# Weight splits on VectorE instead of GpSimd outside DeltaNet's heads two to six, and a new order at the end of DeltaNet and of GLA

## The chip, the cores and the metric

The kernel runs on one core of a Trainium2 chip. The metric is the device time of one execution in microseconds (us); of several executions the median counts. The engines are TensorE (PE, matrix products; PEld is its weight loading), VectorE (DVE), ScalarE (ACT), GpSimd (POOL) and SyncE (SP), which issues the DMAs. Each engine works off its own queue in order.

## The reference, cut to what matters

Two transformer-like blocks run one after the other in float32 over 256 tokens (stream x) and 256 context tokens (stream c) of width 1024. The first block has two layers of attention with a Fourier and a convolution branch. The second has a DeltaNet layer and a GLA layer. Each layer ends with a feed-forward network of width 4096.

```python
h = modulate(rms_norm(x, g), shift, scale)       # for x and for ctx
# DeltaNet, 8 heads: q, k, v, z, a, b = h @ w_in (q, k, v through a short convolution)
for d in range(2):                               # forward and backward in time
    oc, state = gated_delta_rule(qc, kc, vc, ...)      # context first
    ox, _     = gated_delta_rule(qx, kx, vx, ..., state)
y = (rms_norm(o, norm_g) * silu(z)) @ w_out      # per head, then summed over heads
# GLA, 4 heads: the same with a gated linear recurrence, results for x alone
x = x + gate * y
x = x + gate2 * (square(relu(modulate(rms_norm(x, g2), ...) @ w1)) @ w2)
```

## The kernel before

*Products in two halves.* Every float32 weight tile of 128x1024 numbers arrives by DMA (`wr`), ACT casts it to a shortened format (`wh`, line 307), and DVE or POOL subtracts that from the original to get the rest (`wl`, line 308, "the split"). The activations are split likewise (line 295). A product is then three matmuls per 128 rows of the depth, so 24 for one weight tile over eight depth blocks: high by high, high by low, low by high (lines 316 to 318; they are 512 columns wide for both streams, 256 for one). Raw tiles have three buffers, `wh` and `wl` two each, and four in the feed-forward blocks.

*Who splits.* `weight(pool=True)` puts the split on POOL, and so does `self.pool_lo`, which `pools` sets for the whole of DeltaNet. Of the calls outside DeltaNet these have `pool=True`: the first four weights of each of the four feed-forward blocks (line 561), the two first weights of each mixer that `follow` loads ahead, and six weights at GLA's start.

*DeltaNet.* The mixer runs head by head, in a software pipeline written out by hand. In iteration `hd`: `merge` (inverts the head's triangular matrices), `steps` (four steps of the recurrence over chunks of 128 tokens; the context's two chunks are final after the second), `prepare` and `tokens` for the next head, `write_out` of the head before (its product with `w_out`, added to the running sum `xs` by `finish`, line 659), `scale` (sum of squares on ACT, then a reciprocal root on DVE in some ten short operations, lines 432 to 438, and a multiplication of the results `ot`, line 1416), `project` two heads ahead, and `readout` (transposes of `ot` on PE, a multiplication by the gates, a split), then `gates` of the next head. In the last iteration there is nothing left to prepare, so `late` makes 24 small parts of three matmuls each: the last head's second gate and the write-out of head seven. `between` hands one or two of them out between the matmuls of `merge` and `steps`; the rest runs after `scale` is issued. Then `readout`, and `write_out` for head eight, one stream after the other, with each stream's norm for the feed-forward block behind it (`then`, the `follow` function).

*GLA.* It runs by heads as well: `values` and the gate logits of the next head, `readout` of the head before, `gate` and `prepare` of the next head, then `finish` of this one, which makes the output in a PSUM tile `po` (one buffer), scales it into `ot` (one buffer, line 1676). The last `readout` is issued inside the final output product (`tail`).

*Order.* On each engine the instructions stand in an order that the framework plans before the run from the program's order and its own estimates of durations. `self.tc.issue_after(i)` keeps what is issued under it behind instruction i in that plan. The hardware then waits by semaphores only.

Of the kernel before, what the change touches and what calls it, by code (L numbers as in the profile page):

```python
# [204 lines left out]
class Net:  # L205
# [91 lines left out]
    def weight(self, src, into=None, pool=False, ahead=False):  # L297
        shp = list(src.shape)
        raw = self.wp.tile(shp, F32, tag="wr", bufs=self.nr_, name="wr")
        self.nc.sync.dma_start(raw, src)  # L300
        wp, nw = (self.wp2, 4) if self.wp2 and not ahead else (self.wp, self.nw)
        if into:
            hi, lo = into
        else:
            hi = wp.tile(shp, F32R, tag="wh", bufs=nw, name="wh")
            lo = wp.tile(shp, F32R, tag="wl", bufs=nw, name="wl")
        self.nc.scalar.copy(hi, raw)  # L307
        (self.nc.gpsimd if pool or self.pool_lo else self.nc.vector).tensor_tensor(lo, raw, hi.bitcast(F32), ALU.subtract)  # L308
        return hi, lo
# [10 lines left out]
    def lin(self, src, rhs, n0, n1, w=None, pool=False):  # L320
        w = w or self.weight(src, pool=pool)
        ps = self.mm_ps()
        self.mm3(ps[:, : n1 - n0], w, rhs, n0, n1)
        return ps[:, : n1 - n0]
# [194 lines left out]
    def follow(self, f, xs, S, gs, mod, shch, tag, win=None):  # L519
        f.update(h=self.rows16(), ws=None)  # L520

        def then(sv, y=None):
            if win and not f["ws"]:
                f["ws"] = [self.weight(w, pool=True, ahead=True) for w in win]
# [28 lines left out]
    def ffn(self, xs, g, w1, w2, mod, tag, streams, ys=None, h=None, quota=0, every=1, S=None, scales=None, before=None, then=None):  # L553
        one = len(streams) == 1
        with ExitStack() as st:
            self.pools(st, dict(n=(8, 256), h=3, acc=(4, 256), sq=(4, 256), rs=(1, 258)), dict(a=2, md=1, mm=5), 12 if one else 18, "a", quota)
            self.wp2 = self.lo
            if S is not None:
                S.update(acc={}, new=lambda n: self.t("acc", n), tmp=lambda n: self.t("sq", n))
            self.load_ahead(1)  # L560
            ws = [self.weight(self.a[w1][m], pool=True) for m in range(4)]
            self.background(1 if every == 2 else 0)
            self.load_ahead()
            self.every, self.slots = every, 0
            nS = None
# [4 lines left out]
            self.mlp(xs, h, ws, w1, w2, mod, 5, streams, S, scales or {"xc"[v]: 1.0 for (_, _, v) in streams}, before, then, nS)  # L570
            self.background(999)
            self.wp2 = None


    def mlp(self, xs, h, ws, w1, w2, mod, gch, streams, S, scales, before, then, nS):
        nc = self.nc
        n = 256 * len(streams)
        for s in range(4):
# [3 lines left out]
            for m in range(0, 8, 2):  # L582
# [88 lines left out]
    def pools(self, st, sb, ps, nr, pm, quota=0, pool_lo=False, nwm=2, wide=4, low=()):  # L671
        self.n += 1
        self.pool_lo = pool_lo
# [394 lines left out]
    def deltanet(self, xs, mod, h, ws, first):  # L1068
# [249 lines left out]
        def merge(hd, c, parts):  # L1318
# [30 lines left out]
        def steps(hd, c, parts):  # L1349
# [4 lines left out]
            for step in range(4):  # L1354
                Sn = ap.tile([P, 512], F32, tag="S", bufs=2, name="S") if step < 3 else None
                for d in range(2):
# [31 lines left out]
                    self.between(parts, i.ins, 2 if step == 3 else 1)  # L1388
# [13 lines left out]
                S = Sn  # L1402
            return ot

        def scale(c, ot):
            ss = sp.tile([P, 4, 2], F32, tag="ss", name="ss")
            jk = junk()
            for ch in range(4):
                for v in range(2):
                    nc.scalar.activation(jk, ot[ch // 2][:, 256 * (ch % 2) + P * v : 256 * (ch % 2) + P * v + P], AF.Square,  # L1410
                                         accum_out=ss[:, ch, v : v + 1])
            nc.vector.scalar_tensor_tensor(ss, ss, 1.0 / 128, c["aq"].unsqueeze(2).to_broadcast([P, 4, 2]), ALU.mult, ALU.add)
            so = self.rsqrt(ss.rearrange("p c v -> p (c v)"), [P, 8], "o")
            for p in range(2):
                o = ot[p].rearrange("p (c i) -> p c i", i=P)
                nc.vector.tensor_tensor(o, o, so[:, 4 * p : 4 * p + 4].unsqueeze(2).to_broadcast([P, 4, P]), ALU.mult)
# [11 lines left out]
        def write_out(hd, og, S=None, then=None):  # L1428
            ws = [self.weight(a["dwout"][hd, mq]) for mq in range(2)]
            for sv in st if S else [(0, 512, 0)]:  # L1430
                for m in range(8):
                    c = slice(P * (m % 4), P * (m % 4) + P)
                    wh, wl = ws[m // 4]
                    ps = self.mm_ps()[:, : sv[1] - sv[0]]
                    self.mm3(ps, (wh[:, :, c], wl[:, :, c]), og, sv[0], sv[1])
                    if S:
                        self.finish(xs, m, ps, mod, 2, sv, S, dict(x=1.0, c=1.0))
                    else:
                        for s2 in st:
                            self.finish(xs, m, ps[:, s2[0] : s2[1]], mod, 2, s2, None, None)  # L1440
                if then:
                    then(sv)
# [5 lines left out]
        og, parts = None, iter(())  # L1448
        for hd in range(8):
            if hd == 7:  # L1450
                parts = late(zs, og)
            merge(hd, c, parts)
            ot = steps(hd, c, parts)
            if hd < 7:
                nxt = prepare(hd + 1, *proj)
            if 0 < hd < 7:
                write_out(hd - 1, og)
            if hd < 7:
                tokens(nxt)
# [4 lines left out]
            elif hd == 6:  # L1464
                zn = [gate(7, 0)]
# [5 lines left out]
            if hd < 6:  # L1471
                zs = gates(hd + 1)
            elif hd == 6:
                zs = zn
            if hd < 7:
                c = nxt
# [4 lines left out]
        write_out(7, og, S, f["then"])  # L1481
# [4 lines left out]
    def gla(self, xs, mod, h, ws):  # L1486
# [46 lines left out]
        w3 = self.weight(win[2], [vtile().rearrange("p b n -> p (b n)").rearrange("p (k m) -> p k m", k=8).bitcast(F32R) for _ in range(2)], pool=True)  # L1533
# [5 lines left out]
        for m in range(4):  # L1539
            ps = self.lin(win[1 + m], h, 0, 512, w3 if m == 1 else None, True) if m else ps1  # L1540
# [6 lines left out]
        for m in range(4):  # L1547
            ps = self.lin(win[5 + m], h, 0, 256, None, m<3)
# [7 lines left out]
        def values(hd):  # L1556
            w = [self.weight(a["gwv"][hd, kh], pool=False) for kh in range(2)]
# [15 lines left out]
        def gate(hd):  # L1573
            zs = []
            for m in range(2):
                ps = self.lin(win[9 + 2 * hd + m], h, 0, 256, None, False)
# [121 lines left out]
        for hd in range(4):  # L1698
            if hd < 3:
                vn = values(hd + 1)  # L1700
                c1 = next(cg)
            if ot is not None:
# [6 lines left out]
            if hd < 3:  # L1709
                cur, vt, zs = nxt, vn, zn  # L1710

        def last():
            with self.tc.issue_after(self.mark.ins):
                og.extend(readout(3, ot, zo))
# [8 lines left out]
    def run(self):  # L1723
# [8 lines left out]
        if not skip:  # L1732
            fng = None
            y = None
            for l in range(2):
                with ExitStack() as st:
# [7 lines left out]
                    if l == 0:  # L1744
# [34 lines left out]
                        def early():  # L1779
                            self.background(2)  # L1780
                            ws = [self.weight(a["win_0"][m], pool=False) for m in (8, 9)]
# [24 lines left out]
                else:  # L1806
# [3 lines left out]
                    def before(s):  # L1810
# [6 lines left out]
                        if s == 2.5:  # L1817
# [4 lines left out]
                            f["ws"] = [self.weight(a["dwin"][m], pool=True, ahead=True) for m in range(2)]  # L1822
# [40 lines left out]
        with ExitStack() as st:  # L1863
            self.pools(st, dict(g=3, e=(5, 256)), dict(b=2, a=3, mm=3), 4, "b", pool_lo=True)
# [10 lines left out]
        self.ffn(xs, "fg_0", "f1_0", "f2_0", mods2[0][0], "4", both, None, h, 12, 4, S, None, before, lambda sv: f["then"](sv))  # L1875
        self.dump("slay0", xs)
        with ExitStack() as st:
            h = 256
            sb = dict(n=(6, h), low=1, k=4, q=(4, h), z=(4, h), kE=(2, h), kt=(2, h), S=(4, h), qe=(4, h), Ao=(1, h), part=2, A=(2, P), ot=1)
# [42 lines left out]
```

## Time and profile before

| | |
|---|---|
| median of 3 runs | 2655.13 us (2652.54 to 2656.1) |
| profiled execution | 2648.67 us |
| its span | 2646.9 us |
| mean granted clock of PE | 0.977 of full speed |
| PE busy | 2503.5 us, 95% |
| DVE busy | 1648.9 us, 62% |
| ACT busy | 1133.1 us, 43% |
| POOL busy | 370.3 us, 14% |

The profile is of one execution, recorded by the hardware; its span lies within that execution's time. "Busy" is the union of the recorded instructions on an engine. Matmuls overlap in the records, so their mean duration is longer than the distance from one to the next. PEclk is the clock that PE was granted as a share of full speed, 2.4 GHz; 0.5 is the lower level, 1.2 GHz. On the time axis the first block takes about 0 to 1000 us, DeltaNet 1000 to 1852, its feed-forward block up to 2240, GLA 2248 to 2448 and the last feed-forward block the rest.

### The profile page before, as it was taken

What the parts mean: (1) busy time and instruction counts of PE and PEld (TensorE: products, weight loads), DVE (VectorE), ACT (ScalarE), POOL (GpSimd) and SP (SyncE); (2) the same over time, 40 slices, a digit from 0 to 9 for tenths busy, and PEclk for the clock granted to TensorE, in tenths of its full rate; (3) what the DMA queues carried; (4) which work ended last, traced back from release to release, by engine and by line L of the source; (5) the groups of instructions that cost most, each with busy time, mean ns of one, the idle gap of its engine ahead of it and who ended that gap; (6) DMA issues with size and microseconds to landing.
All of it is one profiled execution on the core that took longest, in us unless ns stands there. A gap on an engine that the chain in (4) does not pass through costs nothing. (4 is left out here: it accounts for less than half of the span.)

```text
span 2646.9 us, 40579 instructions
## 1 busy us (share of the span) xinstructions
PE 2503.5 (95%) x15740; PEld 2108.8 (80%) x15740; DVE 1648.9 (62%) x3449; ACT 1133.1 (43%) x2161; POOL 370.3 (14%) x268
## 2 busy tenths in 40 slices
PE   7999999999999999988999999977999999899999
PEld 4866877778886999867778877866877888698899
DVE  5555443333567777887877887767533435677676
ACT  3344333232355545663545444534422324564453
POOL 0000200000100100332333323312000001420100
PEclk8999999999999999999999999988999999999999
DMA  7334566663241466222122211211554522222554
GB/s 266 120 117 147 176 254 236 242 236 117 77 141 52 160 194 197 80 66 53 34 61 65 71 39 52 65 35 56 204 179 160 182 88 71 79 93 73 172 184 154
DMA packets 147105, 334.09 MB, mean 126 GB/s; under 512 B 57134, under 2 KB 68512, under 8 KB 146912
## 3 DMA queue, kind: packets, MB, share of 16 engines
q1 hardware_dynamic: 146656, 331.43, 38.6%
q8 instruction: 124, 2.03, 0.3%
q14 instruction: 69, 0.57, 0.1%
q0 software_dynamic: 256, 0.07, 0.0%
HBM read 327.78 MB, written 3.67 MB: 125 GB/s over the span
## 5 line engine op out<-in xcount | busy, mean ns | idle before, releaser
L307 ACT CAST wh<-wr 128x1024 fp32r<-128x1024 f32 (+1 forms) x421 | 426.1, 1016 | 700.2 <-PE pmm L317 511.4
L318 PE MATMUL pmm<-h,wl 128*128 128x512 f32 (+2 forms) x1800 | 624.6, 347 | 16.3 <-DVE wl L308 8.8
L316 PE MATMUL pmm<-h,wh 128*128 128x512 f32 (+2 forms) x1800 | 628.8, 349 | 6.9 <-ACT E L829 1.9
L317 PE MATMUL pmm<-h,wh 128*128 128x512 f32 (+2 forms) x1800 | 621.3, 345 | 0.0
L308 DVE TENSOR_TENSOR wl<-wr,wh 128x1024 fp32r<-128x1024 f32 (+1 forms) x333 | 392.3, 1180 | 288.8 <-ACT wh L307 282.3
L318 PE MATMUL pmm<-r,wl 128*128 128x256 f32 (+1 forms) x1312 | 444.3, 339 | 5.6 <-DVE wl L308 5.5
L316 PE MATMUL pmm<-r,wh 128*128 128x256 f32 (+1 forms) x1312 | 444.9, 340 | 4.5 <-DVE q L989 1.6
L317 PE MATMUL pmm<-r,wh 128*128 128x256 f32 (+1 forms) x1312 | 444.2, 339 | 0.1
L308 POOL TENSOR_TENSOR wl<-wr,wh 128x1024 fp32r<-128x1024 f32 x88 | 216.5, 2465 | 1383.1 <-ACT wh L307 724.4
L318 PEld LDWEIGHTS pmm<-h,wl 128*128 128x128 f32 x1800 | 346.6, 193 | 59.7 <-DVE wl L308 10.2
L316 PEld LDWEIGHTS pmm<-h,wh 128*128 128x128 f32 x1800 | 346.3, 192 | 53.0 <-issue 7.2
L317 PEld LDWEIGHTS pmm<-h,wh 128*128 128x128 f32 x1800 | 346.7, 193 | 37.1 <-issue 0.8
L316 PEld LDWEIGHTS pmm<-r,wh 128*128 128x128 f32 x1312 | 248.4, 190 | 38.7 <-issue 8.9
L318 PEld LDWEIGHTS pmm<-r,wl 128*128 128x128 f32 x1312 | 248.8, 190 | 32.0 <-DVE wl L308 7.0
L317 PEld LDWEIGHTS pmm<-r,wh 128*128 128x128 f32 x1312 | 249.1, 190 | 23.2 <-issue 1.7
L659 DVE SCALAR_TENSOR_TENSOR xs<-pmm,modb,xs 128x256 f32<-128x256 f32 x232 | 106.6, 477 | 133.0 <-PE pmm L318 133.0
L659 DVE SCALAR_TENSOR_TENSOR xs<-pmm,moda,xs 128x256 f32<-128x256 f32 x120 | 54.4, 480 | 146.7 <-PE pmm L318 146.5
L294 ACT CAST r<-h 128x256 fp32r<-128x256 f32 (+1 forms) x128 | 65.5, 513 | 126.8 <-DVE h L610 67.2
L295 DVE TENSOR_TENSOR r<-h,r 128x256 fp32r<-128x256 f32 (+1 forms) x128 | 72.9, 570 | 44.1 <-ACT r L294 40.7
L394 PE MATMUL pmd<-wm,cvs 128*32 128x256 f32 x1408 | 87.2, 382 | 0.0
L1371 ACT COPY e<-pa 128x256 f32<-128x256 f32 x64 | 23.8, 371 | 128.5 <-PE pa L1369 128.0
L394 PEld LDWEIGHTS pmd<-wm,cvs 128*32 128x32 f32 x1408 | 41.1, 109 | 40.1 <-issue 13.4
(484 smaller groups left out, 3834.7 us busy)
## 6 DMA issues: line engine op xcount, KB each, us to landing
wr<-w SPq DMA_DIRECT2D x128, 512.0 KB
wr<-f SPq DMA_DIRECT2D x128, 512.0 KB
wm<-amod SPq DMA_DIRECT2D x24, 2048.0 KB
wr<-dwin SPq DMA_DIRECT2D x49, 512.0 KB
wm<-wmod SPq DMA_DIRECT2D x12, 2048.0 KB
wr<-win SPq DMA_DIRECT2D x28, 512.0 KB
wm<-wmod SPq DMA_DIRECT2D x8, 1536.0 KB
wr<-gwin SPq DMA_DIRECT2D x17, 512.0 KB
```

Source lines behind the costliest of these rows:

```text
L294: self.nc.scalar.copy(hi, src)
L295: self.nc.vector.tensor_tensor(lo, src, hi.bitcast(F32), ALU.subtract)
L307: self.nc.scalar.copy(hi, raw)
L308: (self.nc.gpsimd if pool or self.pool_lo else self.nc.vector).tensor_tensor(lo, raw, hi.bitcast(F32), ALU.subtract)
L316: mm(ps, wh[:, k, :], rh[:, n0:n1], start=k == 0, stop=False)
L317: mm(ps, wh[:, k, :], rl[:, n0:n1], start=False, stop=False)
L318: self.mark = mm(ps, wl[:, k, :], rh[:, n0:n1], start=False, stop=k == last)
L394: self.last = nc.tensor.matmul(ps[32 * c : 32 * c + 32, :256], cs[:, k + i, :], raw[:, i, 256 * c : 256 * c + 256], start=k + i == 0, stop ...
L659: self.nc.vector.scalar_tensor_tensor(x, ps, mod[:, 8 * gch + m, v : v + 1], x, ALU.mult, ALU.add)
L1371: nc.scalar.copy(vA, ptr[:, :256])
```

## The change

The argument `pool` of `weight` and `lin` goes, with all uses. `pool_lo` is no longer a property of a stage: it is false, and DeltaNet's loop sets it for its second to sixth iteration. DeltaNet's last head stands behind the loop. Both its gates are projected in the iteration before, ahead of the `readout`. `late` holds only the write-out of head seven, 16 parts for `merge` and the rest; `steps` takes parts only in its first two steps, one at a time. After the second step the context's results are scaled (`half`), after the last one the other stream's; `readout1` and `write_last` work on one stream, the context first. The feed-forward block behind it begins its first products with the context too (`order`). In GLA the gates of the last head come behind its `finish`, the `readout` of the head before behind them, and `ot` has two buffers.

```diff
-    def weight(self, src, into=None, pool=False, ahead=False):
+    def weight(self, src, into=None, ahead=False):
...
-        (self.nc.gpsimd if pool or self.pool_lo else self.nc.vector).tensor_tensor(lo, raw, hi.bitcast(F32), ALU.subtract)
+        (self.nc.gpsimd if self.pool_lo else self.nc.vector).tensor_tensor(lo, raw, hi.bitcast(F32), ALU.subtract)
...
-            ws = [self.weight(self.a[w1][m], pool=True) for m in range(4)]
+            ws = [self.weight(self.a[w1][m]) for m in range(4)]
...
-                    first = self.lins(ws[:4], h, streams)
+                    first = self.lins(ws[:4], h, order)
...
-        self.pool_lo = pool_lo
+        self.pool_lo = False
...
-        def late(zs, og):
-            def use(ps):
-                zs.append(ap.tile([P, 512], F32, tag="vf", bufs=2, name="z"))
-                nc.scalar.activation(zs[1], ps, AF.Silu)
-
-            yield from self.lin_parts(lambda: self.weight(win[48]), h, 512, use)
+        def late(og):
...
-                    self.between(parts, i.ins, 2 if step == 3 else 1)
+                    if step < 2:
+                        self.between(parts, i.ins)
...
                 S = Sn
+                if step == 1 and half:
+                    half(ot)
             return ot
...
-        def scale(c, ot):
-            ss = sp.tile([P, 4, 2], F32, tag="ss", name="ss")
+
+        def scale(c, ot, streams=(0, 1)):
+            n = len(streams)
+            ss = sp.tile([P, 2 * n, 2], F32, tag=f"ss{n}", name="ss")
...
+        def readout1(ot, zs, og, p):
+            pt = self.b_ps()
+            sl = slice(256 * p, 256 * p + 256)
+            for v in range(2):
+                for j in range(2):
+                    self.transpose(pt[:, C(2 * v + j)], ot[p][:, 256 * j + P * v : 256 * j + P * v + P])
+            for v in range(2):
+                z = zs[v][:, sl]
+                nc.vector.scalar_tensor_tensor(z, pt[:, 256 * v : 256 * v + 256], dng[:, 0:1], z, ALU.mult, ALU.mult)
+                self.split(og[v][0][:, sl], og[v][1][:, sl], z)
...
+        def write_last(ws, og, sv, S):
+            for m in range(8):
+                c = slice(P * (m % 4), P * (m % 4) + P)
+                ps = self.mm_ps()[:, :256]
+                self.mm3(ps, [w[:, :, c] for w in ws[m // 4]], og, sv[0], sv[1])
+                self.finish(xs, m, ps, mod, 2, sv, S, dict(x=1.0, c=1.0))
...
+        for hd in range(7):
+
+
+            self.pool_lo = 0 < hd < 6
+            merge(hd, c)
+            ot = steps(hd, c)
+            nxt = prepare(hd + 1, *proj)
+            if hd:
                 write_out(hd - 1, og)
-            if hd < 7:
-                tokens(nxt)
+            tokens(nxt)
             scale(c, ot)
...
-                for part in parts:
-                    part()
+                zn = gates(7)
             with self.tc.issue_after(self.mark.ins):
                 og = readout(ot, zs)
...
+        parts = late(og)
+        merge(7, c, parts)
+        ot = steps(7, c, parts, lambda ot: scale(c, ot, (1,)))
+        scale(c, ot, (0,))
...
+        readout1(ot, zs, og, 1)
+        for part in parts:
+            part()
+        ws = [self.weight(a["dwout"][7, mq]) for mq in range(2)]
+        write_last(ws, og, st[1], S)
+        with self.tc.issue_after(self.mark.ins):
+            readout1(ot, zs, og, 0)
+        f["then"](st[1])
+        write_last(ws, og, st[0], S)
+        f["then"](st[0])
...
-            if hd < 3:
-                zn = gate(hd + 1)
-                nxt = prepare(hd + 1, *c1, vn)
+
+            if hd < 2:
+                zn = gate(hd + 1)
+            nxt = prepare(hd + 1, *c1, vn)
             ot, zo = finish(hd, vt, *cur), zs
-            if hd < 3:
-                cur, vt, zs = nxt, vn, zn
+            cur, vt, zs = nxt, vn, zn
+        o3 = finish(3, vt, *cur)
+        zs = gate(3)
+        with self.tc.issue_after(self.mark.ins):
+            og += readout(2, ot, zo)
...
-            self.pools(st, dict(g=3, e=(5, 256)), dict(b=2, a=3, mm=3), 4, "b", pool_lo=True)
+            self.pools(st, dict(g=3, e=(5, 256)), dict(b=2, a=3, mm=3), 4, "b")
```

## Rows read from the trace of the kernel before

**Rows 1.** The page: busy time of each engine, share of the span, instructions.

```profile
PE 2503.5 (95%) x15740; PEld 2108.8 (80%) x15740; DVE 1648.9 (62%) x3449; ACT 1133.1 (43%) x2161; POOL 370.3 (14%) x268
```

**Rows 2.** Stretches: length; PE, PEld, DVE, ACT, POOL busy (instructions); PEclk; DMA share; GB/s.

```profile
875.00:895.00 20.00, 15.98 (x105) 15.50 (x104) 14.56 (x30) 9.43 (x15) 10.57 (x4) 0.83 0.55 183
1094.00:1262.00 168.00, 145.75 (x768) 118.73 (x766) 133.16 (x265) 87.74 (x189) 62.96 (x36) 0.93 0.23 63
1740.00:1852.00 112.00, 80.36 (x457) 67.30 (x455) 74.09 (x172) 40.97 (x106) 21.19 (x9) 0.85 0.17 48
2250.00:2330.00 80.00, 67.42 (x393) 57.73 (x394) 56.05 (x93) 48.20 (x62) 35.92 (x30) 0.91 0.27 81
```

**Rows 3.** Line 308: duration in ns, least/median/greatest; first and last start.

```profile
L308 DVE TENSOR_TENSOR wl<-wr,wh x333: 409/1225/3355, 50.7 to 2635.3; 128x1024 fp32r<-128x1024 f32 x155, 128x384 fp32r<-128x384 f32 x8, 128x256 fp32r<-128x256 f32 x4
...
L308 POOL TENSOR_TENSOR wl<-wr,wh x88: 2338/2404/3402, 286.8 to 2461.8; 128x1024 fp32r<-128x1024 f32 x88
```

**Rows 4.** Timeline, 878 to 879 us: start, us, engine, line, operation, [idle before <- releaser].

```profile
878.11 0.28 PE L317 MATMUL pmm<-h,wh 128*128 128x256 f32 x1
...
878.23 0.28 PE L318 MATMUL pmm<-h,wl 128*128 128x256 f32 x1
...
878.49 2.39 POOL L308 TENSOR_TENSOR wl<-wr,wh 128x1024 fp32r<-128x1024 f32 x1 [18.11 <-ACT wh L307]
...
878.76 2.41 DVE L477 TENSOR_TENSOR xs<-xs,sq 128x256 f32<-128x256 f32 x1 [0.80 <-ACT sq L475]
```

**Rows 5.** Line 477: durations as in rows 3.

```profile
L477 DVE TENSOR_TENSOR xs<-xs,sq x7: 418/420/2410, 868.1 to 888.2; 128x256 f32<-128x256 f32 x7
```

**Rows 6.** Waits of PE, 1094 to 1262: line, releaser, us in total, times, longest.

```profile
PE pmm L318 <- POOL wl L308: 4.7, 1, 4.7
...
PE pb L452 <- DVE vt L1312: 2.8, 1, 2.8
```

**Rows 7.** Timeline, 1146 us.

```profile
1146.16 2.56 DVE L1255 TENSOR_TENSOR Mt<-Mt,g 128x256 f32<-128x256 f32 x1
```

**Rows 8.** Timeline, 1721 to 1725 us.

```profile
1721.46 2.36 DVE L1395 TENSOR_TENSOR ot<-ot,e 128x256 f32<-128x256 f32 x1
...
1724.13 0.49 PE L1369 MATMUL pa<-e,TT 128*128 128x128 f32 x2 [1.64 <-DVE e L1365]
```

**Rows 9.** Timeline, 1749 to 1753 us.

```profile
1749.69 2.34 POOL L308 TENSOR_TENSOR wl<-wr,wh 128x1024 fp32r<-128x1024 f32 x1 [6.83 <-ACT wh L307]
1749.73 3.45 DVE L1416 TENSOR_TENSOR ot<-ot,rsy 128x512 f32<-128x512 f32 x2
...
1752.73 0.66 PE L452 MATMUL pb<-k_id,ot 128*128 128x128 f32 x2 [5.91 <-DVE ot L1416]
```

**Rows 10.** Line 1416: durations.

```profile
L1416 DVE TENSOR_TENSOR ot<-ot,rsy x16: 678/684/2928, 1265.1 to 1830.1; 128x512 f32<-128x512 f32 x16
```

**Rows 11.** Timeline, 1820 to 1831 us.

```profile
1820.18 9.25 POOL L308 TENSOR_TENSOR wl<-wr,wh 128x1024 fp32r<-128x1024 f32 x4 [2.30 <-ACT wh L307]
1820.42 2.13 DVE L438 SCALAR_TENSOR_TENSOR rsy<-rst,rsy 128x8 f32<-128x8 f32 x1
...
1827.18 2.27 DVE L438 SCALAR_TENSOR_TENSOR rsy<-rst,rsy 128x8 f32<-128x8 f32 x1
...
1830.23 1.12 PE L452 MATMUL pb<-k_id,ot 128*128 128x128 f32 x4 [11.25 <-DVE ot L1416]
```

**Rows 12.** Line 436: durations.

```profile
L436 DVE TENSOR_TENSOR rst<-rsy x123: 142/161/2261, 45.2 to 2466.7; 128x2 f32<-128x2 f32 x63, 128x4 f32<-128x4 f32 x36, 128x8 f32<-128x8 f32 x24
```

**Rows 13.** Busy time, 1812 to 1852, as in rows 2.

```profile
1812.00:1852.00 40.00, 24.93 (x148) 22.57 (x146) 33.42 (x79) 18.30 (x44) 14.02 (x6) 0.79 0.25 79
```

**Rows 14.** Waits of PE, 2395 to 2434, as in rows 6.

```profile
PE pgt L452 <- DVE ot L1676: 3.9, 2, 2.7
```

**Rows 15.** Timeline, 2451 to 2455 us.

```profile
2450.98 3.35 DVE L308 TENSOR_TENSOR wl<-wr,wh 128x1024 fp32r<-128x1024 f32 x1
...
2454.39 0.58 PE L318 MATMUL pmm<-r,wl 128*128 128x256 f32 x1 [4.40 <-DVE wl L308]
```

More of the change, by code (lines that the diff above doesn't have):

```diff
@@ L318, in mm3, with lin @@
             self.mark = mm(ps, wl[:, k, :], rh[:, n0:n1], start=False, stop=k == last)
-    def lin(self, src, rhs, n0, n1, w=None, pool=False):
-        w = w or self.weight(src, pool=pool)
+    def lin(self, src, rhs, n0, n1, w=None):
+        w = w or self.weight(src)
         ps = self.mm_ps()
@@ L523, in then @@
             if win and not f["ws"]:
-                f["ws"] = [self.weight(w, pool=True, ahead=True) for w in win]
+                f["ws"] = [self.weight(w, ahead=True) for w in win]
             self.norm_one(f["h"], xs, sv, gs, mod, shch, y or self.stat_end(S, "xc"[sv[2]]), tag, True)
@@ L549, in residual, with ffn @@
                                                 xs[:, m, c0:c1], ALU.mult, ALU.add)
-    def ffn(self, xs, g, w1, w2, mod, tag, streams, ys=None, h=None, quota=0, every=1, S=None, scales=None, before=None, then=None):
+    def ffn(self, xs, g, w1, w2, mod, tag, streams, ys=None, h=None, quota=0, every=1, S=None, scales=None, before=None, then=None, order=None):
         one = len(streams) == 1
@@ L569, in ffn, with mlp @@
                 h = self.norm_mod(xs, streams, self.gscale(mod, 4, g, tag), mod, 3, ys, "n", self.hr(), True)
-            self.mlp(xs, h, ws, w1, w2, mod, 5, streams, S, scales or {"xc"[v]: 1.0 for (_, _, v) in streams}, before, then, nS)
+            self.mlp(xs, h, ws, w1, w2, mod, 5, streams, S, scales or {"xc"[v]: 1.0 for (_, _, v) in streams}, before, then, nS, order or streams)
             self.background(999)
             self.wp2 = None
-    def mlp(self, xs, h, ws, w1, w2, mod, gch, streams, S, scales, before, then, nS):
+    def mlp(self, xs, h, ws, w1, w2, mod, gch, streams, S, scales, before, then, nS, order):
         nc = self.nc
@@ L667, in finish, with pools @@
                 S["next"](m)
-    def pools(self, st, sb, ps, nr, pm, quota=0, pool_lo=False, nwm=2, wide=4, low=()):
+    def pools(self, st, sb, ps, nr, pm, quota=0, nwm=2, wide=4, low=()):
         self.n += 1
-        self.pool_lo = pool_lo
+        self.pool_lo = False
         self.wp2 = None
@@ L1315, in tokens, with merge @@
             c["vt"] = vt
-        def merge(hd, c, parts):
+        def merge(hd, c, parts=iter(())):
             Mt, TT = c["Mt"], c["TT"]
@@ L1346, in merge, with steps @@
                     nc.vector.tensor_tensor(mix(TT[1], 4 * hf, 4, s), v4(FT), v4(pzt), ALU.subtract)
-        def steps(hd, c, parts):
+        def steps(hd, c, parts=iter(()), half=None):
             kq, vt, D, mbt, ktm, TB = c["kq"], c["vt"], c["D"], c["mbt"], c["ktm"], c["TT"][1]
@@ L1447, in deltanet @@
         proj = project(1)
[L1448 to L1453, printed above, removed]
-            if hd < 7:
-                nxt = prepare(hd + 1, *proj)
-            if 0 < hd < 7:
+        og = None
+        for hd in range(7):
[4 more added lines that the diff above has]
+            if hd:
                 write_out(hd - 1, og)
-            if hd < 7:
-                tokens(nxt)
+            tokens(nxt)
             scale(c, ot)
@@ L1463, in deltanet @@
                 proj = project(hd + 2)
-            elif hd == 6:
-                zn = [gate(7, 0)]
-            else:
-                for part in parts:
-                    part()
+            else:
+                zn = gates(7)
             with self.tc.issue_after(self.mark.ins):
                 og = readout(ot, zs)
[L1471 to L1476, printed above, removed]
+            zs = gates(hd + 1) if hd < 6 else zn
+            c = nxt
+        parts = late(og)
+        merge(7, c, parts)
+        ot = steps(7, c, parts, lambda ot: scale(c, ot, (1,)))
+        scale(c, ot, (0,))
+        D = lambda: ap.tile([P, 4, P], F32, tag="D", bufs=8, name="og").rearrange("p s i -> p (s i)").bitcast(F32R)
+        og = [(D(), D()) for _ in range(2)]
         S = dict(acc={}, new=lambda n: ap.tile([P, 512], F32, tag="FT", bufs=2, name="acc")[:, :n],
@@ L1530, in gates @@
                 yield cums, tots
-        w3 = self.weight(win[2], [vtile().rearrange("p b n -> p (b n)").rearrange("p (k m) -> p k m", k=8).bitcast(F32R) for _ in range(2)], pool=True)
+        w3 = self.weight(win[2], [vtile().rearrange("p b n -> p (b n)").rearrange("p (k m) -> p k m", k=8).bitcast(F32R) for _ in range(2)])
         ps, ps1 = self.lins(ws, h, st)
@@ L1556, in values @@
         def values(hd):
-            w = [self.weight(a["gwv"][hd, kh], pool=False) for kh in range(2)]
+            w = [self.weight(a["gwv"][hd, kh]) for kh in range(2)]
             vs = vtile()
@@ L1780, in early @@
                             self.background(2)
-                            ws = [self.weight(a["win_0"][m], pool=False) for m in (8, 9)]
+                            ws = [self.weight(a["win_0"][m]) for m in (8, 9)]
                             self.background(5)
@@ L1821, in before @@
                             f["gs"] = gs
-                            f["ws"] = [self.weight(a["dwin"][m], pool=True, ahead=True) for m in range(2)]
+                            f["ws"] = [self.weight(a["dwin"][m], ahead=True) for m in range(2)]
                         if s == 3.5:
@@ L1878, in run @@
             h = 256
-            sb = dict(n=(6, h), low=1, k=4, q=(4, h), z=(4, h), kE=(2, h), kt=(2, h), S=(4, h), qe=(4, h), Ao=(1, h), part=2, A=(2, P), ot=1)
+            sb = dict(n=(6, h), low=1, k=4, q=(4, h), z=(4, h), kE=(2, h), kt=(2, h), S=(4, h), qe=(4, h), Ao=(1, h), part=2, A=(2, P), ot=2)
             self.pools(st, sb, dict(gt=2, ad=2, po=1, mm=3), 4, "gt")
```

54 lines of the change are left out of this document (23 added, 31 removed).

## The prediction, made before the change had run

> **What bounds the kernel now.** The page's busy shares come first: TensorE (PE) is busy 2503.5 us, 95% of the span, VectorE (DVE) 1648.9, GpSimd (POOL) 370.3 [rows 1]. What DVE or POOL does can cost time only where PE stands idle or runs at the lower clock. So the second view is the busy time by stretches; to be read there is a stretch's length less PE's busy time, and PEclk. Where PEclk is c, the clock stood at 1.2 instead of 2.4 GHz for 2(1 - c) of the stretch; a half-clock spell costs up to half its length where PE was full in it, and nothing where PE waited anyway. Idle and half clock, in us [rows 2]: 875 to 895: 4.0 and 6.8; DeltaNet's prologue and first head, 1094 to 1262: 22.3 and 23.5; its last head, 1740 to 1852: 31.6 and 33.6; GLA's start, 2250 to 2330: 12.6 and 14.4. That is 70.5 idle and, at half price, 39 of clock; with two waits of 3.9 and 4.40 us further on, some 118 us is the most that can come back.
>
> Third, the split itself. The same 128x1024 subtraction has a median of 1.225 us on DVE and 2.404 on POOL [rows 3].
>
> Fourth, what POOL does to DVE. At 878.76 a subtraction of two SBUF tiles took 2.41 us on DVE beside a POOL split that ran from 878.49 to 880.88 [rows 4]; the same operation has a median of 0.420 [rows 5]. It lost 2.0 us. Each engine's queue is in order, so all that stood behind it on DVE was late by as much. Last come PE's waits by releaser, stretch by stretch; where DVE is named, the timeline beside it shows what had held DVE.
>
> **The change, part by part.** Fifty-one of POOL's 91 splits (88 in rows 3, three in tiles of other names) go to DVE: 28 outside DeltaNet (four at each of four feed-forward (FFN) entries, two ahead of each of three mixers, six inside GLA) and 23 in DeltaNet (prologue and first head 15, last two heads 8). The 40 in the iterations of heads two to six stay. DVE gets 51 x 1.225 = 62.5 us of work; POOL loses 51 x 2.40 = 122.4. What DVE gets back lies between nothing (no split meets a two-input operation) and 122 (each locks it throughout). Where they meet, rows show 2.0 or more lost; I take that for two splits in three: 51 x 2/3 x 2.0 = 68. So DVE's load hardly changes on balance, and only places where something waited count.
>
> *875 to 895.* The blocked subtraction delays the weight split behind it, on which PE stood. Half of the 4.0 idle: 2 (0 to 5). At the first FFN's entry near 300 I see no wait behind a POOL split: 0 (-1 to 1).
>
> *Prologue and first head.* PE's long waits here: 4.7 us for a POOL split and 2.8 for a tile that DVE made late [rows 6], DVE having stood in a multiplication of 2.56 us beside a POOL split [rows 7]. With the split on DVE the first gets 4.7 - 1.2 = 3.5 shorter, if the split isn't queued behind other work; for the second I take 1.5. Of the half clock (at most 11.8) I take 2. Sum 7. DVE was busy 133.2 of 168 us [rows 2]; 15 splits add 18.4, and if nothing came back it would stand at 152, nearly full: low end -8 (somewhat under half of that added work turning up as waits), high end 15.
>
> *Heads two to six.* A head loses 1.64 us to a DVE operation that took 2.36 us, where the like in rows 5 takes 0.42 [rows 8]. Their splits stay; only the iteration that ends them (head seven, whose splits move) gets its share: 1 (0 to 2).
>
> *Last head, start.* PE stood 5.91 us for two scalings of 3.45 us [rows 9], one of which stood beside a POOL split (median 0.684, longest 2.928) [rows 10]. Both gates of the last head now come ahead of the readout: 24 matmuls of 512 columns more, at twice the 0.12 us spacing of the 256-column ones in rows 4 about 5.8 us, which fills the hole. They were fillers of merge and steps, where 16 remain of 24; I take 3 as given back there. Net 5 - 3 = 2 (-3 to 5). SP's load of that gate weight moves ahead of two output weights by the same step; DMA stands at 0.17 of its time there [rows 2], which hides it.
>
> *Last head, end.* The longest wait of all: 11.25 us, since operations on 128x8 numbers took 2.13 us and more (four in a row, of which the first and the last are shown; median of such: 0.161) while POOL made the FFN's four splits in 9.25 us [rows 11, 12]. On DVE these are 4.9 us. Also the context stream is scaled during the last two steps, so PE has its write-out (48 x 0.12 = 5.8 us) and six left-over parts (4.1 us of 18 matmuls) while the other stream is scaled. The new wait, the second readout behind that write-out, holds back only the second write-out, which needs it. By PE's work alone about 20 would go. Against it stands DVE: busy 33.4 us between 1812 and 1852 [rows 13], of which 4 x 2.0 were blocked, so 25, plus 7.4 for six splits; a part falls behind the FFN's start, since one stream is normed under the other's matmuls. I estimate that the FFN begins some 30 us after the steps instead of 40: 10 (3 to 20).
>
> *GLA.* Start: PE is idle 12.6 us; six splits add 7.4 to DVE's 56 of 80: 2 (-3 to 8). End: PE waited 3.9 us in two waits, the longer 2.7, for the scaled results of heads three and four [rows 14]. The last head's gates (48 x 0.12 = 5.8 us) now stand ahead of the last readout and cover the 2.7. The other stays: the output's PSUM tile is still one, and head four's results need it scaled free. With some clock 3; but these gates covered the preparation of that head before: -4 to 7.
>
> *Entry to the last FFN.* PE waited 4.40 us for a DVE split of 3.35, which should take 1.2 [rows 15]; two POOL splits stood beside it. Four FFN splits join DVE's queue instead: 4 (0 to 7).
>
> Sum: 2 + 7 + 1 + 2 + 10 + 2 + 3 + 4 = 31. The profiled execution took 2648.67 us (span 2646.9), so its like would take 2617.7. It lies 6.5 under the median of the runs shown, 2655.13: the forecast is 2624.
>
> A rule of the Trainium skill speaks against the move: "Perfetto Trace Analysis" (Optimizing Scalar/DVE Operations) holds that with a saturated DVE it may pay to hand work to GpSimd, with the caveat that the two share a port. "SBUF — State Buffer" (SBUF: two separate sides) calls that port an exclusive lock for a whole instruction. By the first half, the prologue's splits would cost their full 18.4 us; by the lock, little. The row at 878.76 agrees with the lock; no row of the stretches has DVE saturated.
>
> **Rivals.**
> 1. *Only the reordering counts.* POOL's splits were mostly hidden, and DVE's queue delivers them no earlier. For it: PE hardly waits on a POOL split by name. Against: rows 4, 11 and 15, where POOL is the cause unnamed. Last head 8, GLA's end 3: 11 us, 2644.
> 2. *DVE becomes the bound (slower).* In prologue and first head, last two heads and GLA's start 15 + 8 + 6 = 29 splits stand in DVE's in-order queue ahead of operations of the recurrences on which PE waits, and no lock time comes back: 29 x 1.225 = 35.5 lost, 11 gained: 24 slower, 2680. It decides once DVE's work fills a stretch, 168 us in the prologue against the 152 above; rows 7 and 11, where lock time must come back, speak against it.
> 3. *The clock comes back too.* With the waits of the last head and the prologue go the half-clock spells that began in them: prologue 15, last head 26, GLA 10, the rest 8: 59, so 2596. Against: DVE's 32 us between steps and FFN.
> 4. *It doesn't do what it says:* the instructions are ordered so that the wait before the last readout stays. 31 - 10 = 21: 2634, inside the forecast's range.
>
> **How the numbers follow.** Forecast, 2609 to 2636 (rival 4 in it): 0.60. Rival 1: 0.17; rival 3: 0.14; rival 2: 0.07; small losses at several places: 0.02. The 80% range takes in rival 1 and the nearer half of rival 3: 2600 to 2646. About 0.2% (5 us) is what a measurement of this kernel can tell from no change. Faster: 0.60 + 0.14 and nearly all of rival 1: 0.88; same 0.05; slower 0.07.
>
> **What would show it.** Right: POOL's busy time falls to about 250 us and DVE's stays within 15 of 1649; no short DVE operation takes over 2 us outside heads two to six; the 11.25 us wait comes under 3, and the FFN starts some 10 us nearer to the steps' end; the wait at the last FFN's entry is under 1. Wrong: DVE busy 40 us more, new waits of PE for DVE splits in prologue and GLA, heads two to six changed in length, or new waits in the last head's steps for want of fillers.

## The result and the profile after

The changed kernel takes 2612.25 us (median of 4 runs, 2609.9 to 2615.09), the one before 2653.84 beside it: ratio 0.9843, 95% interval 0.9826 to 0.986, so 41.6 us faster. The forecast was 2624 (2600 to 2646). The profiled execution took 2609.9 us, its span 2608.1.

The page after, busy times, which answers to [rows 1]:

```profile
PE 2493.9 (96%) x15740; PEld 2100.2 (81%) x15740; DVE 1649.7 (63%) x3517; ACT 1136.4 (44%) x2165; POOL 237.1 (9%) x217
```

GpSimd lost 133 us of work, VectorE took over 51 splits, some 62 us, and is as busy as before (1649.7 against 1648.9). The time that its operations had spent blocked has paid for the splits.

Where the 38.8 us between the two spans came from is read by following the same PE product through both traces: its start before less its start after, and how that difference grows from one place to the next. (The last column is the sixth experiment below, the fourth and fifth columns the first two.)

| stretch of the kernel before, us | forecast | after | splits only | order only | after, old addresses |
|---|---|---|---|---|---|
| 0 to 870 | 0 | -3.1 | -1.4 | -2.7 | -0.9 |
| 870 to 930, second FFN entry | 2 | -0.7 | -0.9 | 0.1 | -0.3 |
| 930 to 1088 | not priced | 1.4 | 1.1 | 0.5 | 0.9 |
| 1088 to 1262, prologue, first head | 7 | 15.7 | 15.9 | -0.3 | 16.1 |
| 1262 to 1689, heads two to six | 0 | -4.0 | 0.0 | -3.7 | -0.3 |
| 1689 to 1900, last two heads, FFN start | 13 | 17.7 | 13.3 | 4.1 | 17.9 |
| 1900 to 2345, FFN, GLA's start | 2 | 3.2 | 3.0 | 0.9 | 1.3 |
| 2345 to 2440, GLA's end | 3 | 4.5 | -0.2 | 4.7 | 4.3 |
| 2440 to the end, last FFN's entry | 4 | 3.8 | 4.3 | 0.1 | 4.8 |

Stretches after, the columns as in [rows 2]. The first holds the same 768 products as the row for 1094 to 1262 there, the second is DeltaNet's end:

```profile
1097.80:1248.60 150.80, 138.35 (x768) 113.06 (x766) 127.18 (x275) 88.78 (x189) 25.31 (x20) 0.98 0.26 72
1784.00:1821.00 37.00, 26.63 (x169) 24.41 (x167) 35.09 (x114) 21.10 (x56) 2.19 (x3) 0.88 0.23 72
```

In the prologue PE's idle time fell from 22.3 to 12.5 us and the half-clock time from 23.5 to 6.0 (2 x 0.02 x 150.8). DVE is busy 6.0 us less there although it has the splits: without these 15 x 1.2 us, its other operations take 24 us less than before. Two of PE's waits of before (1094 to 1262) that are gone, and then its longest wait after (1097.8 to 1248.6) and what is left of the one for `vt` in [rows 6]:

```profile
PE pb L1245 <- ACT g L1239: 3.2, 1, 3.2
PE pb L1245 <- DVE row L1152: 2.1, 1, 2.1
```

```profile
PE pmm L318 <- DVE wl L308: 4.2, 1, 4.2
PE pb L452 <- DVE vt L1307: 1.7, 1, 1.7
```

The 4.2 us are the wait for the split of which [rows 6] has 4.7: it hardly got shorter. The split's weight was cast by 1178.87 at the latest, but the split stood behind other work in DVE's queue:

```profile
1177.82 1.05 ACT L307 CAST wh<-wr 128x1024 fp32r<-128x1024 f32 x1
...
1182.73 1.21 DVE L308 TENSOR_TENSOR wl<-wr,wh 128x1024 fp32r<-128x1024 f32 x1
```

PE's waits after, 1715 to 1845, which answer to [rows 9, 11], and its rows at the last FFN's entry, which answer to [rows 15]:

```profile
PE pmm L350 <- DVE xs L659: 7.1, 1, 7.1
PE pb L452 <- DVE ot L1417: 4.3, 1, 4.3
PE pa L1328 <- DMA TT<-dout: 3.3, 1, 3.3
```

```profile
2414.91 0.39 PE L316 MATMUL pmm<-r,wh 128*128 128x256 f32 x1 [1.72 <-ACT wh L307]
2416.38 0.58 PE L318 MATMUL pmm<-r,wl 128*128 128x256 f32 x1 [0.97 <-DVE wl L308]
```

The 11.25 us wait for the scaled results is 4.3, and the 5.91 us one is gone; instead the FFN's first product waits 7.1 us, since DVE works through residuals, norms and splits without a pause (35.09 of 37 us). The 4.40 us wait for a split is 0.97.

At the second FFN entry a wait of PE grows from 1.6 to 4.29 us (before, 875 to 895; then after on DVE, ACT and PE):

```profile
PE pt L446 <- DVE xs L477: 1.6, 1, 1.6
```

```profile
890.10 1.22 DVE L308 TENSOR_TENSOR wl<-wr,wh 128x1024 fp32r<-128x1024 f32 x1 [1.14 <-ACT wh L307]
891.24 0.42 DVE L477 TENSOR_TENSOR xs<-xs,sq 128x256 f32<-128x256 f32 x1
```

```profile
889.02 1.04 ACT L307 CAST wh<-wr 128x1024 fp32r<-128x1024 f32 x1 [1.71 <-DMA wr<-w]
889.97 0.41 ACT L475 ACTIVATE sq<-xs 128x256 f32<-128x256 f32 x1
```

```profile
891.81 0.34 PE L446 MATMUL pt<-ones,xs 128*128 128x1 f32 x1 [4.29 <-DVE xs L477]
```

A split waits 1.14 us at the head of DVE's queue for a weight that isn't cast yet; the addition behind it, on which the norm and PE wait, had its data at 890.38 and starts 0.86 us later. On GpSimd the split's wait held up nobody. The square that the addition needs is late too: in ACT's queue it stands behind the same weight's cast, which waited 1.71 us for its DMA.

### The profile page after: what moved, and what is told of

It reads as the page before. It is cut to its first block, busy times and chain, and to the rows that moved or that the text cites. A ratio compares the mean times of both kernels' runs of the same rounds, so it can differ in the third digit from the quotient of the medians.

```text
span 2608.1 us, 40590 instructions
## 1 busy us (share of the span) xinstructions
PE 2493.9 (96%) x15740; PEld 2100.2 (81%) x15740; DVE 1649.7 (63%) x3517; ACT 1136.4 (44%) x2165; POOL 237.1 (9%) x217
## 4 chain that ended last, share of the span: by engine, by line
PE 80%; DVE 10%; issue 5%; ACT 3%; DMA 2%; POOL 1%; SPq 0%; DVEq 0%; ACTq 0%; POOLq 0%
PE pmm L316 20%; PE pmm L318 19%; PE pmm L317 19%; PE pmd L394 3%; PE ps L1004 1%; DVE wl L308 1%; PE pmm L351 1%; DMA wm<-wmod 1%; PE pa L1364 1%; PE pmm L352 1%; PE pmm L350 1%; PE pa L1382 1%; PE pa L1340 1%; PE pv L1042 1%; ACT wh L307 1%
## 5 line engine op out<-in xcount | busy, mean ns | idle before, releaser
L308 DVE TENSOR_TENSOR wl<-wr,wh 128x1024 fp32r<-128x1024 f32 (+1 forms) x381 | 449.4, 1181 | 314.8 <-ACT wh L307 307.9
L316 PE MATMUL pmm<-r,wh 128*128 128x256 f32 (+1 forms) x1280 | 436.1, 342 | 4.1 <-ACT wh L307 2.3
L318 PE MATMUL pmm<-r,wl 128*128 128x256 f32 (+1 forms) x1280 | 435.0, 341 | 2.5 <-DVE wl L308 2.4
L317 PE MATMUL pmm<-r,wh 128*128 128x256 f32 (+1 forms) x1280 | 433.8, 339 | 0.0
L316 PEld LDWEIGHTS pmm<-h,wh 128*128 128x128 f32 x1800 | 342.5, 190 | 55.2 <-issue 7.2
L317 PEld LDWEIGHTS pmm<-h,wh 128*128 128x128 f32 x1800 | 343.0, 191 | 39.5 <-issue 0.8
L316 PEld LDWEIGHTS pmm<-r,wh 128*128 128x128 f32 x1280 | 241.3, 189 | 37.0 <-issue 8.9
L318 PEld LDWEIGHTS pmm<-r,wl 128*128 128x128 f32 x1280 | 241.5, 189 | 28.9 <-DVE wl L308 3.9
L317 PEld LDWEIGHTS pmm<-r,wh 128*128 128x128 f32 x1280 | 241.8, 189 | 22.7 <-issue 1.7
L516 POOL TENSOR_TENSOR h<-n,h 128x256 fp32r<-128x256 f32 x28 | 21.7, 775 | 1154.3 <-ACT h L515 1154.3
L308 POOL TENSOR_TENSOR wl<-wr,wh 128x1024 fp32r<-128x1024 f32 x40 | 96.2, 2405 | 146.7 <-ACT wh L307 112.9
L295 DVE TENSOR_TENSOR r<-h,r 128x256 fp32r<-128x256 f32 (+1 forms) x128 | 71.2, 557 | 42.0 <-ACT r L294 39.5
```

The lines of the kernel that those rows point to most:

```text
L295: self.nc.vector.tensor_tensor(lo, src, hi.bitcast(F32), ALU.subtract)
L308: (self.nc.gpsimd if self.pool_lo else self.nc.vector).tensor_tensor(lo, raw, hi.bitcast(F32), ALU.subtract)
L316: mm(ps, wh[:, k, :], rh[:, n0:n1], start=k == 0, stop=False)
L317: mm(ps, wh[:, k, :], rl[:, n0:n1], start=False, stop=False)
L318: self.mark = mm(ps, wl[:, k, :], rh[:, n0:n1], start=False, stop=k == last)
```

## The experiments

Theory A: GpSimd's splits locked VectorE, and that lock, not the splits' own duration, was the price. Rivals: B, only the new order counts; C, VectorE's queue is the bound. A further rival, that a split is done sooner on VectorE because it takes 1.2 us there and not 2.4, has no run of its own; the prologue's wait for a split, 4.7 us before and 4.2 after, speaks against it there.

The runs below stood beside the kernel before in different rounds. Differences from the changed kernel are taken between medians; by the ratios to the kernel before they come out up to 2.2 us otherwise.

**1. Splits only** and **2. order only.** The two halves of the change, alone.

```diff
# splits only: the kernel before, and
-(self.nc.gpsimd if pool or self.pool_lo else self.nc.vector).tensor_tensor(lo, raw, ...)
+(self.nc.gpsimd if self.pool_lo else self.nc.vector).tensor_tensor(lo, raw, ...)
+            self.pool_lo = 0 < hd < 6      # in the loop over heads
# order only: the changed kernel, and GpSimd for all 91 splits
```

> The order of the kernel before, with the 51 splits on VectorE as in the changed kernel. Theory A (GpSimd's splits locked VectorE's two-input operations, and the prologue's 16 us came back by that): prologue 16, GLA's start 3, entry to the last feed-forward block 4, the prologue's loaded-ahead weights 1, a part of the 11.25 us wait at DeltaNet's end 6, less 1 at the second feed-forward entry: 29 us faster than before, 24 to 33. Rival B (only the new order counts): within 5 us of before.

> The new order at the end of DeltaNet and GLA, with all 91 splits on GpSimd as before. Theory A: what is left of the 41.6 us after the splits' 29, so 12 us faster than before, 8 to 17. Rival B: 35 to 42 us faster than before.

Splits only: 2614.61 us, ratio 0.9852 (0.9837 to 0.9867), 39.1 faster than before. Order only: 2647.79, 0.9981 (0.9971 to 0.9991), 5.9 faster. B has fallen; the splits brought more than the 24 to 33 us that A had, the order less than its 8 to 17. Added to the splits, the order is worth 2.4 us (2614.61 less 2612.25), which the two intervals don't tell from nothing; experiments 6 and 7 show what took back its gain. What a split costs the chain of the reciprocal root on either engine is seen by holding [rows 11] against the splits-only kernel:

```profile
1797.32 0.15 DVE L436 TENSOR_TENSOR rst<-rsy 128x8 f32<-128x8 f32 x1
1797.39 1.21 DVE L308 TENSOR_TENSOR wl<-wr,wh 128x1024 fp32r<-128x1024 f32 x1
1798.53 0.15 DVE L437 TENSOR_TENSOR rst<-rst,rsh 128x8 f32<-128x8 f32 x1
1798.61 1.21 DVE L308 TENSOR_TENSOR wl<-wr,wh 128x1024 fp32r<-128x1024 f32 x1
1799.74 0.15 DVE L438 SCALAR_TENSOR_TENSOR rsy<-rst,rsy 128x8 f32<-128x8 f32 x1
```

Here too a split stands between every two links, but a link takes 1.2 us and not 2.3. PE's longest wait for `ot` becomes 6.3 us by that alone; with the new order alone it is 8.0 (PE's waits, splits only from 1690 to 1830, then order only from 1730 to 1860):

```profile
PE pb L452 <- DVE ot L1416: 9.9, 2, 6.3
```

```profile
PE pb L452 <- DVE ot L1417: 8.4, 2, 8.0
```

**3. The 51 splits left out.**

```diff
# in weight, for the 51 weights
+        if skip or self.skip:
+            return hi, hi
```

> The changed kernel with the 51 moved splits left out on any engine (the product takes the high half twice): VectorE has 62.5 us less to do than in the changed kernel. Theory A (VectorE has room nearly everywhere, so the splits cost it little where they now stand): 8 to 14 us faster than the changed kernel, of it 7 at DeltaNet's end, where VectorE is full, and 2 at the second feed-forward entry. Rival C (VectorE's queue has become the bound, and the splits are paid in full): 30 us or more faster than the changed kernel.

2605.03 us (runs from 2601.29 to 2612.16), 7.2 faster than the changed kernel and just under the 8 to 14 that A had (0.9819 of before, 0.9803 to 0.9835), VectorE busy 1593.5 us. C has fallen: 62 us of added work cost about 7. I expected these at DeltaNet's end, and that is a miss: its FFN starts only 1.8 us sooner (1821.47 against 1823.27), with the wait there still 6.5 us. Between the profiled runs (5.1 us apart in span) this kernel gains more than the changed one at the second FFN entry (3.7 us), in the prologue and first heads (17.3 instead of 14.7 from 1088 to 1345, a place behind the prologue where the products stand in the same order again) and at GLA's start (3.4). Against that it loses 4.5 us between 740 and 830, where PE ran at the lower clock for a while (PEclk from 700 to 870 is 0.97, in the changed kernel 1.00); why there stays open.

**4. The other 40 splits on VectorE too.**

```diff
-            self.pool_lo = 0 < hd < 6
```

> The changed kernel with the last 40 GpSimd splits, those of DeltaNet's heads two to six, on VectorE as well. Theory A: each of the five heads loses its 1.6 us stall beside a GpSimd split, VectorE's load stays: 6 to 9 us faster than the changed kernel. Rival C (VectorE at 80% of a head, splits queue ahead of the recurrence's operations): 5 to 15 us slower than the changed kernel.

2600.64 us, ratio 0.9797 (0.9782 to 0.9811), 11.6 faster than the changed kernel, more than the 6 to 9 that A had; C, which had it slower, has fallen here too. PE's waits in the heads, changed kernel first (1256 to 1679), then this one (1250 to 1675):

```profile
PE pa L1364 <- DVE e L1360: 6.8, 5, 1.6
PE pa L1340 <- DVE Y L1331: 3.8, 4, 1.0
```

```profile
PE pa L1335 <- DVE Y L1331: 6.0, 9, 0.7
PE pa L1371 <- DVE e L1369: 0.9, 1, 0.9
```

The 1.6 us wait of each head is gone, and a head is 83.6 us long instead of 86.8. The splits that the change leaves on GpSimd are what it leaves unused.

**5. The prologue's 15 splits back on GpSimd.**

```diff
-            self.pool_lo = 0 < hd < 6
+            self.pool_lo = hd < 6          # and true from the stage's start
```

> The changed kernel with the 15 splits of DeltaNet's prologue and first head back on GpSimd. Theory A: the stretch's whole gain of 16 us hangs on them: 14 to 17 us slower than the changed kernel. Rival (the prologue's term as I priced it, the rest of the stretch's gain from elsewhere, such as the weights loaded ahead): 7 us slower.

2626.48 us, 0.9905 (0.9891 to 0.9918), 14.2 slower than the changed kernel; the stretch 1088 to 1262 gains -0.2 instead of 15.7. All of its gain hangs on these 15 splits.

**6. Old addresses** and **7. new addresses alone.** From 0 to 870 and in heads two to six the changed kernel loses 7 us where it changes next to nothing; the order-only kernel loses them too, the splits-only kernel far less. There, PE's 512-column products follow one another every 232 ns instead of 227. The new order's small tiles (`ss1`, `ss2`, `rsyo1`, `rsyo2`) enlarge their pool, and by the order in which the kernel allocates its pools the tiles behind it, the mixers' activations among them, lie 128 bytes higher, while the mixers' weight tiles stay.

```diff
# old addresses: the changed kernel, and
-ss = sp.tile([P, 2 * n, 2], F32, tag=f"ss{n}", name="ss")
+ss = sp.tile([P, 4, 2], F32, tag="ss", name="ss")[:, : 2 * n]
# (the root's tile likewise); new addresses: the kernel before, and
+nc.vector.memset(self.sp.tile([P, 16], F32, tag="pad", name="pad"), 0.0)
```

> The changed kernel, in which the new small tiles share the tags of the old ones, so that the small tile pool has its old size and all tiles behind it lie 128 bytes lower, where they lay before. Theory L (512-column products of the mixers take 232 ns instead of 227 because their operands lie 128 bytes higher): the pace is 227 ns again and the kernel is 6 to 7 us faster than the changed one, about 2606. Rival (the slower pace comes from the order of instructions): no difference, 2612.

> The kernel before with one unused small tile of 64 bytes in two buffers more, which moves the tiles behind by 128 bytes and changes nothing else. Theory L: the pace of 512-column products goes from 227 to 232 ns, 5 to 7 us slower than before. Rival: no difference.

Old addresses: 2604.34 us, 0.9819 (0.9806 to 0.9833), 7.9 faster than the changed kernel. New addresses alone: 2659.57, 1.0027 (1.0017 to 1.0037), 6.6 slower than before. Starts of two products with 26 between them, changed kernel, then old addresses:

```profile
1391.94 0.40 PE L316 MATMUL pmm<-h,wh 128*128 128x512 f32 x1
...
1398.21 0.40 PE L316 MATMUL pmm<-h,wh 128*128 128x512 f32 x1
```

```profile
1391.91 0.39 PE L316 MATMUL pmm<-h,wh 128*128 128x512 f32 x1
...
1398.03 0.39 PE L316 MATMUL pmm<-h,wh 128*128 128x512 f32 x1
```

27 steps take 6.27 us, or 232 ns each, and 6.12, or 227. Why an address does that stays open.

**8. Zeros instead of the prologue's splits.** As experiment 5, and

```diff
+        if self.zero:                      # prologue and first head
+            self.nc.gpsimd.memset(lo.bitcast(F32), 0.0)
+            return hi, lo
```

> As the kernel with the prologue's 15 splits back on GpSimd, but GpSimd only writes zeros into the low halves and reads nothing (the low halves of these weights are left out). If GpSimd locks VectorE only when it reads SBUF: no operation of VectorE with two SBUF inputs over 2 us in the prologue, and the stretch as short as in the changed kernel or up to 5 us shorter. If any GpSimd operation locks it: VectorE's operations are still longer beside the zeros, by the zeros' duration, and the stretch is 5 to 15 us longer than in the changed kernel.

2614.90 us (0.985, 0.9832 to 0.9867); up to 1345 the stretch gains 13.9 us, in the changed kernel 14.7. Two of GpSimd's writes beside VectorE's operations, and then the first of these operations in the kernel before, with GpSimd idle and, on 128x169 numbers, beside a split:

```profile
1164.29 0.95 POOL L309 MEMSET wl<- 128x1024 f32 x1 [4.63 <-PE pmm L321]
...
1164.47 0.50 DVE L1273 TENSOR_TENSOR lf<-lf,XX 128x196 f32<-128x196 f32 x1
```

```profile
1119.19 0.42 DVE L1148 CAST g<-g 96x512 bf16<-96x512 f32 x1 [0.61 <-issue]
...
1120.15 0.95 POOL L309 MEMSET wl<- 128x1024 f32 x1 [9.03 <-PE pmm L321]
...
1120.56 0.81 DVE L1148 CAST g<-g 96x512 bf16<-96x512 f32 x1
```

```profile
1746.11 0.50 DVE L1275 TENSOR_TENSOR lf<-lf,XX 128x196 f32<-128x196 f32 x1
```

```profile
1173.49 2.36 POOL L308 TENSOR_TENSOR wl<-wr,wh 128x1024 fp32r<-128x1024 f32 x1 [5.49 <-ACT wh L307]
1173.80 2.37 DVE L1275 TENSOR_TENSOR lf<-lf,XX 128x169 f32<-128x169 f32 x1
```

Beside the write the two-input operation takes its usual 0.50 us, while a split holds it up (2.37 us, where 128x169 numbers take 0.47 at 1745.24 with GpSimd idle); the cast is held up by the write too, 0.81 us instead of the 0.42 just before. So writing alone doesn't lock a two-input operation, but does hold a cast.

**9 to 12. Put together.** `best1` is the changed kernel with experiments 4 and 6 and one edit for the second FFN entry; `best2` also takes DeltaNet's remaining two-input work off GpSimd; `best3` takes the norms' low halves instead; `best2_64` is `best2` with the tiles moved by 64 bytes.

```diff
# best1: in the feed-forward blocks of one stream
-ws = [self.weight(self.a[w1][m]) for m in range(4)]
+ws = [self.weight(self.a[w1][m]) for m in range(3)]
+with self.tc.issue_after(self.held.ins) if one else ExitStack():   # the last residual's operation
+    ws.append(self.weight(self.a[w1][3]))
# best2: best1, and
-nc.gpsimd.tensor_tensor(Mt[:, ch], Dc[:, 0:2], Dc[:, 2:4], ALU.add)
+nc.vector.tensor_tensor(Mt[:, ch], Dc[:, 0:2], Dc[:, 2:4], ALU.add)
-(nc.gpsimd if ch%2 else nc.vector).tensor_tensor(Dc, Dc, ...)
+nc.vector.tensor_tensor(Dc, Dc, ...)
```

> The changed kernel with three further edits: all splits on VectorE, the small tile pool at its old size, and at the entries of the two one-stream feed-forward blocks the fourth weight's split held behind the last residual's operation on VectorE's queue. If they add up: 2612.3 - 11.6 (all splits) - 7.9 (layout) - 2 (the wait at the second feed-forward entry, 4.29 us in the changed kernel, down to about 2) = 2591. If the held split only moves the wait to the first product: 2593 or more.

> The kernel with the three further edits, and DeltaNet's Mt additions and D multiplications that are still on GpSimd (four and two in a head) on VectorE as well. They are 4 x 0.43 + 2 x 1.15 = 4.0 us of VectorE's time in a head against 4 x 0.73 + 2 x 1.4 = 5.7 us on GpSimd, two thirds of which lock VectorE by theory A: no difference, within 3 us. Rival (any two-input work on GpSimd costs more than it saves here): 5 to 10 us faster, 1 us in a head.

> The kernel with the three further edits, and the low halves of the norms that GpSimd still makes (28 of 0.78 us) on VectorE, where they are 0.42 us each. At DeltaNet's end VectorE is full, and eight of them stand on the path there. Theory A: the lock gives back what they add, within 2 us. Rival C (VectorE's queue): 2 to 4 us slower.

> The fastest kernel so far (all splits and DeltaNet's Mt and D work on VectorE), with one unused small tile of 32 bytes in two buffers, which moves the tiles behind up by 64 bytes instead of 128. If 64 bytes slow the mixers' 512-column products as 128 bytes do: 232 ns, 5 to 8 us slower than that kernel, 2584 to 2587. If the pace at this place is another, it is read from the spacing of the products: 227 ns and 2579 where 64 bytes do no harm, below 2576 where this place is better than both.

| kernel | us | ratio to before | 95% interval |
|---|---|---|---|
| best1 | 2591.46 | 0.9766 | 0.9752 to 0.9781 |
| best2 | 2579.08 | 0.972 | 0.9704 to 0.9737 |
| best3 | 2596.42 | 0.9788 | 0.9774 to 0.9803 |
| best2_64 | 2580.00 | 0.9724 | 0.9708 to 0.974 |

In `best1` the gains add up, though the held split gives little of it: the wait at the second FFN entry is 3.4 us instead of 4.3. What is left is ACT's queue, where the square still stands behind a cast that waits for its DMA (PE's wait, then ACT and DVE):

```profile
PE pt L446 <- DVE xs L477: 3.4, 1, 3.4
```

```profile
886.08 1.04 ACT L307 CAST wh<-wr 128x1024 fp32r<-128x1024 f32 x1 [1.64 <-DMA wr<-w]
...
887.48 0.42 DVE L477 TENSOR_TENSOR xs<-xs,sq 128x256 f32<-128x256 f32 x1 [1.38 <-ACT sq L475]
```

`best2` missed my expectation of no difference by 12 us, to the good and beyond the 5 to 10 of its rival: heads go from 82.9 to 81.5 us, and from 1088 to 1345 it gains 24.3 instead of 16.6. It is the fastest kernel, 74.5 us under before. Its page:

```profile
PE 2478.6 (96%) x15740; PEld 2103.2 (82%) x15740; DVE 1656.0 (64%) x3605; ACT 1135.0 (44%) x2165; POOL 94.4 (4%) x129
```

`best3` is 5 us slower than `best1`. Theory A allowed 2 and rival C had 2 to 4, so here A's expectation fails, though the two intervals overlap: the norms' halves don't gain by the move. In the profiled runs 1.7 us go at the first FFN's norm; why, stays open. With 64 bytes 27 products take 6.18 us, 229 ns each, and no difference in time is measured.

## Why the prediction was right, and which sizes were off

The change does gain by what the prediction names, VectorE's operations freed from GpSimd's splits. That the total came within 12 us of the forecast is partly luck: it would have been nearer 20 without the 7.9 us that the addresses took back, which the prediction didn't know of.

- *VectorE's load hardly changes on balance:* right, 1649.7 us; 62.5 went in, and I had counted on 68 coming back.
- *Prologue and first head, 7:* the term that was mis-sized most; it measured 15.7, and experiment 5 shows that all of it comes from the splits. Its working failed with its size: the 3.5 us from the wait for the split came to 0.5 (4.7 to 4.2), since the split does stand queued behind other work, and the 1.5 from the wait for `vt` to 1.1. The gain came from waits that I hadn't priced, the 3.2 and 2.1 us ones above among them, so that idle time fell by 9.8 us in all, and from the clock: I took 2 of 11.8 us, but the half clock fell by 17.5 us, worth up to 8.8. The low end, DVE nearly full, didn't come near: experiments 3 and 8 show it has room there.
- *Last two heads, 1 + 2 + 10 = 13:* 17.7. The mechanism is right at the end: the FFN starts 28.7 us after the last result of the recurrence instead of 39.5, and I had 30. So the 10 was right (10.8), and the 1 and the 2 in front of it were too low: head seven's iteration fell from 86.1 us to 82.6 (from one scaling of results to the next), and from there to the last result of the recurrence it is 61.6 instead of 66.2. But I had booked much of it to the order; alone, the splits give 13.3 and the order 4.1, which add up to what both give. The 11.25 us wait was to come under 3 us and is 4.3.
- *GLA's end, 3:* 4.5, all of it by the order. *GLA's start, 2:* 3.2. *Last FFN's entry, 4:* 3.8, by the splits.
- *875 to 895, 2:* -0.7. The blocked operation (an addition, not a subtraction) is back at 0.42 us; the step that failed is that a split in DVE's queue waits only for its turn. It waits for its data too, and on ACT a cast did the same. That is rival 2's mechanism, at this place.
- *New waits of PE for DVE's splits in prologue and GLA*, a sign against me, did come, but in place of waits no shorter: 4.2 us for 4.7 in the prologue, and at GLA's start (2246 to 2340 before, 2218 to 2310 after) 9.3 us for splits on either engine instead of 11.0.
- *Heads two to six, 0:* -4.0, and 0 to 870: -3.1. I named a changed head length as a sign against me; its cause is the addresses, which I hadn't considered.

So the sum came out 8 us low: 9 missed in the prologue, 5 at DeltaNet's end, 3 in GLA, 1 ahead of the prologue, less 7 in the stretches of the addresses and 3 at the second entry. The rule of the Trainium skill that speaks for the move's opposite, "Perfetto Trace Analysis" (Optimizing Scalar/DVE Operations), would have cost the prologue 18.4 us if VectorE had been full. The lock that "SBUF — State Buffer" (SBUF: two separate sides) states decides instead, and experiment 8 agrees with its finer point: against a GpSimd operation that reads nothing, the two-input operation isn't blocked (0.50 us).

## What to carry to other kernels

Work on GpSimd isn't free because GpSimd is idle: ask what VectorE does meanwhile, by comparing the durations of one operation with and without GpSimd beside it, and take the clock that the waits cost into the price. Moved to VectorE, the work takes a place in an in-order queue, so see that its data are there when its turn comes, and look at the queue of the engine that makes them too. And when a stretch that the change doesn't touch gets slower at an even rate, look at addresses before looking for a story.

## What the runs showed of the hardware that was not expected

- 128 bytes more in one pool of small tiles slow the mixers' 512-column products from 227 to 232 ns, which cost 6.6 us in one kernel and 7.9 in the other; the feed-forward blocks, whose weights move along, keep 227 ns.
- A GpSimd operation that only writes holds up a cast on VectorE (0.81 us for 0.42) and not an operation with two inputs (0.50 for 0.50), which a split does hold up (2.37 for 0.47).
